# Pinned sums for the conditioning vectors, one operand in PSUM, and weight sums in pieces of 256

## The chip, the cores and the metric

The kernel runs on one core of a Trainium2 chip. The metric is the device time of one execution in microseconds (us). Three timed runs of the kernel before took 3041.25, 3040.60 and 3039.13 us, a median of 3040.6. Line numbers are those of the kernel before, and times within the execution count from the start of its span.

## The reference, cut to what matters

One layer of a denoising backbone runs over 1024 latent and 128 context tokens (1152 columns) of width 1024. Each token passes a first feed-forward half-step, a mixer of attention and a gated scan, and a second feed-forward half-step. Each of the three blocks has a shift, a scale and a gate per channel, nine vectors of 1024 for the latent tokens (from `c`) and nine for the context tokens (from `c_ctx`):

```
mod_p = (jax.nn.silu(c_ctx) @ w_ada[l] + b_ada[l]).reshape(1, N_MOD, D_MODEL)
mod_s = (jax.nn.silu(c) @ w_ada[l] + b_ada[l]).reshape(c.shape[0], N_MOD, D_MODEL)
x = x + 0.5 * m[2] * swiglu(modulate(x, norm_g[0], m[0], m[1]), *ffn1)
x = x + m[5] * mix
x = x + 0.5 * m[8] * swiglu(modulate(x, norm_g[2], m[6], m[7]), *ffn2)
def swiglu(h, w1, w3, w2):
    return (jax.nn.silu(h @ w1) * (h @ w3)) @ w2
```

The products by `w_ada` are matrix-vector products: 9 x 1024 outputs of length 1024, for two vectors. The feed-forward width is 2816, which makes 22 tiles of 128.

## The kernel before, in words

Everything is kept with channels on the partitions and tokens along the free axis. A float32 product is made of three TensorE matmuls on split operands (high by high, high by low, low by high).

Each feed-forward half-step has a way up (`w1`, `w3`, SiLU, product) and a way down (`w2`). In the way up the first tiles (four in the first half-step, three in the second) go through `plain_block`; the rest, 18 and 19 tiles, go through `fast_block`, a scheme with 7 products in place of 8 for each quadrant of weights. This is called the fast stage here. A tile `f` of it has 7 products, each for two column groups (`r`), so 14 blocks of 12 matmuls of 288 columns. Every block ends with an operation on VectorE or ScalarE that empties its PSUM bank (L1544 to L1560). The weights of the 7 products are made in `fast_ops`: GpSimd adds and subtracts 128x512 pieces of the raw weights (L1513, four such sums a tile), ScalarE makes the high part (L1517), VectorE the low part (L1518). Weights are made a few products ahead (the list `made`).

In the way down (`down_group`, `down`), two tiles' weights and hidden values are taken at a time. A group of 24 accumulations (8 output tiles by 3 column chunks of 384) has 6 matmuls for each; VectorE then adds the result, times the gate, to `x` (L481). The PSUM tag `dn` has three banks. ScalarE (L238, L1619) and GpSimd (L239, L1620) split the weights and hidden values of later tiles meanwhile. The last four tiles go through `down_last`.

Conditioning vectors 0 and 1 are made on TensorE at the start. The other seven are made by `ada_sum` on VectorE, beside other work: vectors 2 to 5 in the first fast stage, 6 and 7 in the first way down, 8 in the second fast stage. For each 128x512 block of the transposed `w_ada` (tile `wada`, loaded by L289, two buffers) two SCALAR_TENSOR_TENSOR instructions (L306) multiply it by SiLU of the conditioning row, broadcast over the partitions (tiles `cb`, one for each of the two vectors), and sum along the row into a column of `acc`; a DVE_READ_ACCUMULATOR follows each. This text calls the pair of instructions one sum. There are 128 sums in the first fast stage, 64 in the way down and 32 in the second fast stage.

`ada_sum` is a generator; the loops around it decide where its next step is traced:

```
L1641 if (n in (1, 4)) if l else (7 * f + n) % 3:
L1642     next(ada, None)
```

(after both blocks of product `n`), and in the way down one step after every third accumulation. In the fast stages one step holds both sums of a block of weights; in the way down it holds one. What is traced is not yet the order of the engines: a scheduler orders each engine's queue by its own estimate of when an instruction's operands are there, so an instruction without ties to the work around it can move ahead. `keep_in_program_order` ties an instruction behind the one traced before it on its engine. The queues themselves are in order: SyncE's (SP) issues all the loads and stores named here, and an entry that waits holds those behind it.

Of the kernel before, what the change touches and what calls it, by code (L numbers as in the profile page):

```python
# [9 lines left out]
F32 = mybir.dt.float32  # L10
# [3 lines left out]
AF = mybir.ActivationFunctionType  # L14
ALU = mybir.AluOpType
# [4 lines left out]
P = 128  # L20
D = 1024
# [66 lines left out]
class Trunk:  # L88
# [185 lines left out]
        )  # L274
        self.ada_end(m)

    def ada_sum(self, ms, cb, w2, small, fine=False):

        nc, a = self.nc, self.a
        HD = D // 2  # L280
        acc = small("adac")[:, : 32 * len(ms)].rearrange("p (m h k s) -> p m h k s", m=len(ms), h=2, k=KT)
        junk = small("junk").bitcast(BF16)[:, :HD]
        w2 = w2("wada")
        ws = [w2[:, :HD], w2[:, HD : 2 * HD]]
        units = [(h, i, k) for h in range(2) for i in range(len(ms)) for k in range(KT)]

        def load(n):
            h, i, k = units[n]
            nc.sync.dma_start(ws[n % 2], a["w_aT"][ms[i] - 2, k, :, ts(h, HD)])  # L289

        cs = None
        for n, (h, i, k) in enumerate(units):
            if not i and not k:
                cs = [cb("cb")[:, :HD] for _ in range(2)]
                for s in range(2):
                    nc.sync.dma_start(cs[s], a["cr"][s : s + 1, ts(h, HD)].to_broadcast([P, HD]))
                if not n:
                    load(0)
                for s in range(2):
                    nc.scalar.activation(cs[s], cs[s], AF.Silu)  # L300
                yield
            if n + 1 < len(units):
                load(n + 1)
            for s in range(2):
                o = acc[:, i, h, k, s : s + 1]
                nc.vector.scalar_tensor_tensor(junk, ws[n % 2], 1.0, cs[s], ALU.mult, ALU.mult, accum_out=o)  # L306
                if fine and not s:
                    yield
            if h and k == KT - 1:
                nc.vector.tensor_add(acc[:, i, 0], acc[:, i, 0], acc[:, i, 1])  # L310
                b = self.bada[:, ms[i]].unsqueeze(2).to_broadcast([P, KT, 2])
                nc.vector.tensor_tensor(self.modt[:, ms[i]], acc[:, i, 0], b, ALU.add)
                self.ada_end(ms[i])
            yield
# [1173 lines left out]
    def fast_ops(self, l, fs):  # L1488

        nc = self.nc  # L1490
        raws, n = [None, None], 0

        def load(f, i):
            t = raws[i] = self.wp.tile([P, 2, 512], F32, tag="raw", bufs=2, name="raw")
            for v, (j, h) in enumerate((((0, 0), (1, 0)), ((1, 1), (0, 1)))[i]):
                src = self.a["w13"][l, f, j][:, 4 * h : 4 * h + 4].rearrange("p k m -> p (k m)")
                nc.sync.dma_start(t[:, v], src)

        load(fs[0], 0)
        load(fs[0], 1)  # L1500
        yield
        for j, f in enumerate(fs):
            (a11, a21), (a22, a12) = [(t[:, 0], t[:, 1]) for t in raws]
            s1, s2 = [self.half("ws")[:, :512] for _ in range(2)]
            src = {1: a11, 6: s2, 7: a21, 5: s1, 2: a12, 4: a22, 3: a12}
            pre = {
                6: ((s1, a21, a22, ALU.add), (s2, s1, a11, ALU.subtract)),
                7: ((a21, a11, a21, ALU.subtract),),
                3: ((a12, a12, s2, ALU.subtract),),
            }  # L1510
            for i in PRODUCTS:
                for o, x, y, op in pre.get(i, ()):
                    nc.gpsimd.tensor_tensor(o, x, y, op)  # L1513
                t = self.wp.tile([P, 2, 512], F32R, tag=("wh", "wl")[n % 2], bufs=3, name="wo")
                wh, wl = t[:, 0], t[:, 1]
                n += 1
                nc.scalar.copy(wh, src[i])  # L1517
                nc.vector.tensor_sub(wl, src[i], wh)  # L1518
                if j + 1 < len(fs) and i in (7, 3):
                    load(fs[j + 1], int(i == 3))  # L1520
                yield [w.rearrange("p (k m) -> p k m", k=4) for w in (wh, wl)]
# [42 lines left out]
    def ffn_fast(self, l, gm, nxt):  # L1564

        nc = self.nc
        w2 = self.a["w2"][l]
# [5 lines left out]
        for f in range(plain):  # L1573
            ws = self.pre[f] if l == 0 and f < 2 else [self.load_w(self.a["w13"][l, f, j], KT, P) for j in range(2)]
# [6 lines left out]
            n = 0  # L1581
# [16 lines left out]
        made = [w for w in made if w]  # L1598
        self.B = None
        pend, ws, raws = [], [], []  # L1600
        ada = self.ada_sum((8,) if l else (2, 3, 4, 5), self.half, partial(self.tt, F32), self.slim)
        tile = partial(self.tt, F32) if l == 0 else self.wide
        split = partial(self.wide, dt=F32R) if l == 0 else partial(self.tt, F32R)
        spare = partial(self.tt, F32R) if l == 0 else partial(self.wide, dt=F32R)
# [1 line left out]
        def load_x(k):  # L1606
            t = self.tt(F32, f"x{k}")
            nc.sync.dma_start(t[:, :T], self.xs[k] if l else self.a["xT"][k])
            return t

        def load_h(f):
            raw = tile("hr")[:, :T]
            nc.sync.dma_start(raw, self.hs[f])
            return f, raw

        def split_h(f, raw):
            new = partial(self.tt, F32R) if f in (16, 17) else split
            hh, hl = new(name="hh")[:, :T], new(name="hl")[:, :T]
            nc.scalar.copy(hh, raw)  # L1619
            nc.gpsimd.tensor_sub(hl, raw, hh)  # L1620
            return f, (hh, hl)

        def load_w2(f):
            return self.load_w(w2[f], 1, D, home=spare if f % 2 else None)

        for f in range(plain, NF):
            blocks = [self.fast_block(f, r) for r in range(2)]
            for g in blocks:
                next(g)
            for n in range(7):  # L1630
                if len(made) < 6:
                    w = next(ops, None)
                    if w:
                        made.append(w)
                w = made.pop(0)
                for t in self.puts:
                    self.put(*t)
                self.puts = []
                for g in blocks:
                    g.send(w)  # L1640
                if (n in (1, 4)) if l else (7 * f + n) % 3:  # L1641
                    next(ada, None)  # L1642
                if f == NF - 1:
                    if n == 2:
                        raws = [load_h(0), load_h(1)]
                    elif n == 3:
                        ws.append(load_w2(0))
                        pend.append(split_h(*raws[0]))
                    elif n == 4:
                        pend.append(split_h(*raws[1]))  # L1650
                    elif n == 5:
                        ws.append(load_w2(1))
                        self.x = [load_x(0), load_x(1)]
# [2 lines left out]
            self.put(*t)  # L1656
        self.x += [load_x(k) for k in range(2, KT)]
        if l == 0:
            new = partial(self.tt, F32)
            self.bg = self.ada_sum((6, 7), new, new, self.slim, True)  # L1660
        for f in range(2, NF):
            pend.append(split_h(*load_h(f)))
            if f % 2 and f < NF - 1:
                fs, hs = zip(*pend[:2])
                self.down_group(w2, fs, hs, gm, ws or [load_w2(v) for v in fs])
                pend, ws = pend[2:], None
# [126 lines left out]
```

## Time and profile before

| what | value |
|---|---|
| median of three timed runs | 3040.6 us |
| the profiled execution's own time | 3039.14 us |
| its span, first to last instruction | 3037.4 us |
| mean granted TensorE clock | 0.985 of full speed |
| TensorE matmul busy | 2896.2 us (95%) |
| VectorE busy | 2070.8 us (68%) |
| ScalarE busy | 1233.2 us (41%) |
| GpSimd busy | 1049.2 us (35%) |
| first fast stage | from about 154 to 577 us |
| first way down | from about 577 to 890 us |
| second fast stage | from about 2316 to 2739 us |

TensorE is busy nearly all the time. Time is lost where it waits, and where its granted clock falls, which the records show after some of the waits. The span is 1.7 us shorter than the profiled execution, and that is 1.5 us under the median.

### The profile page before, as it was taken

How to read it: one execution, taken by the hardware profiler on the slowest of the kernel's cores; microseconds unless marked ns; L12 is line 12 of the kernel's file. 1: busy time of each engine (PE TensorE's matmuls, PEld its weight loads, DVE VectorE, ACT ScalarE, POOL GpSimd, SP SyncE). 2: the span in 40 equal slices, each digit the busy share in tenths (PEclk: the TensorE clock that was granted, in tenths of full speed). 3: DMA queues.
4: the chain of work that ended last, by engine and by line, in shares of the span. 5: the costliest groups of instructions: out<-in, count | busy, mean ns of one | idle time of the engine just before them, and what ended most of it. 6: DMA issues, size and time to landing. Idle time of an engine off the chain costs nothing. (4 is left out here: it accounts for less than half of the span.)

```text
span 3037.4 us, 49240 instructions
## 1 busy us (share of the span) xinstructions
PE 2896.2 (95%) x18498; PEld 2743.2 (90%) x18498; DVE 2070.8 (68%) x4206; ACT 1233.2 (41%) x2375; POOL 1049.2 (35%) x831
## 2 busy tenths in 40 slices
PE   7999999989999999999999999989999999999998
PEld 5999999979988988888998778779989999999997
DVE  7787865598668777777636777765675745546665
ACT  5422222211166464555344677751262322332113
POOL 4222222343334233333225444533242222226324
PEclk8999999999999999999999999999999999999999
DMA  6643432553121111111110000143253322226211
GB/s 236 198 152 123 144 108 77 206 198 106 36 96 37 52 38 45 45 45 45 58 60 20 13 17 21 48 149 104 95 188 115 107 75 75 76 93 224 89 44 63
DMA packets 151470, 282.37 MB, mean 93 GB/s; under 512 B 19200, under 2 KB 83648, under 8 KB 151232
## 3 DMA queue, kind: packets, MB, share of 16 engines
q1 hardware_dynamic: 151088, 278.90, 27.7%
q8 instruction: 146, 2.39, 0.3%
q14 instruction: 92, 0.75, 0.1%
q10 hardware_dynamic: 144, 0.33, 0.0%
HBM read 215.64 MB, written 63.52 MB: 92 GB/s over the span
## 5 line engine op out<-in xcount | busy, mean ns | idle before, releaser
L1542 PE MATMUL b<-xo,wo 128*128 128x288 f32 x3552 | 487.1, 297 | 9.6 <-DVE et L1548 9.6
L1542 PEld LDWEIGHTS b<-xo,wo 128*128 128x128 f32 x3552 | 477.3, 189 | 11.5 <-DVE et L1548 11.5
L481 DVE SCALAR_TENSOR_TENSOR x<-dn,modt,x 128x256 f32<-128x256 f32 (+4 forms) x728 | 350.5, 504 | 166.0 <-PE dn L454 164.7
L1542 PE MATMUL b<-bh,wo 128*128 128x288 f32 x1776 | 367.0, 296 | 4.1 <-DVE et L1550 3.2
L239 POOL TENSOR_TENSOR wl<-raw,wh 128x1024 fp32r<-128x1024 f32 (+1 forms) x106 | 241.4, 2278 | 372.9 <-ACT wh L238 357.0
L452 PE MATMUL mm<-xh,wh 128*128 128x384 f32 (+1 forms) x1008 | 362.9, 360 | 5.4 <-DVE q L649 3.1
L454 PE MATMUL mm<-xh,wl 128*128 128x384 f32 (+1 forms) x1008 | 342.9, 340 | 2.0 <-POOL wl L239 1.8
L453 PE MATMUL mm<-xl,wh 128*128 128x384 f32 (+1 forms) x1008 | 343.5, 341 | 0.0
L1542 PEld LDWEIGHTS b<-bh,wo 128*128 128x128 f32 x1776 | 289.9, 189 | 5.8 <-ACT et L1552 5.7
L1542 PE MATMUL b<-bl,wo 128*128 128x288 f32 x888 | 262.2, 295 | 0.0
L452 PE MATMUL dn<-hh,wh 128*128 128x384 f32 (+2 forms) x576 | 199.7, 347 | 23.7 <-DVE x L481 20.7
L306 DVE SCALAR_TENSOR_TENSOR junk<-wada,cb 128x512 bf16<-128x512 f32 x224 | 205.9, 919 | 16.9 <-DMA wada<-in_w_aT 14.5
L238 ACT CAST wh<-raw 128x1024 fp32r<-128x1024 f32 (+1 forms) x108 | 104.3, 967 | 254.8 <-PE dn L453 166.3
L452 PEld LDWEIGHTS mm<-xh,wh 128*128 128x128 f32 (+1 forms) x1008 | 191.1, 190 | 15.3 <-DVE q L649 3.8
L454 PE MATMUL dn<-hh,wl 128*128 128x384 f32 (+2 forms) x576 | 196.0, 340 | 1.0 <-POOL wl L239 1.0
L1517 ACT CAST wo<-raw 128x512 fp32r<-128x512 f32 x185 | 114.0, 622 | 204.1 <-PE b L1542 115.3
L453 PE MATMUL dn<-hl,wh 128*128 128x384 f32 (+2 forms) x576 | 195.4, 339 | 0.0
L454 PEld LDWEIGHTS mm<-xh,wl 128*128 128x128 f32 (+1 forms) x1008 | 190.4, 189 | 3.6 <-POOL wl L239 2.1
L453 PEld LDWEIGHTS mm<-xl,wh 128*128 128x128 f32 (+1 forms) x1008 | 191.6, 190 | 1.6 <-issue 0.4
L1620 POOL TENSOR_TENSOR hl<-hr,hh 128x1152 fp32r<-128x1152 f32 x44 | 120.5, 2747 | 202.9 <-ACT hh L1619 113.6
L1518 DVE TENSOR_TENSOR wo<-raw,wo 128x512 fp32r<-128x512 f32 x185 | 128.2, 694 | 89.6 <-ACT wo L1517 88.9
L1276 POOL TENSOR_TENSOR ehl<-e,ehl 128x512 fp32r<-128x512 f32 x93 | 122.5, 1322 | 141.0 <-ACT ehl L1274 78.2
(384 smaller groups left out, 7140.0 us busy)
## 6 DMA issues: line engine op xcount, KB each, us to landing
raw<-in_w SPq DMA_DIRECT2D x148, 256.0 KB, 2.9
raw<-in_w SPq DMA_DIRECT2D x58, 512.0 KB, 3.6
wada<-in_w_aT SPq DMA_DIRECT2D x112, 256.0 KB, 2.7
hr<-hs SPq DMA_DIRECT2D x44, 576.0 KB, 4.5
hs<-et SPq DMA_DIRECT2D x148, 144.0 KB, 1.7
raw<-in_w_in SPq DMA_DIRECT2D x41, 512.0 KB, 3.5
hb<-hd SPq DMA_DIRECT2D x44, 288.0 KB, 3.5
x<-in_xT SPq DMA_DIRECT2D x16, 576.0 KB, 8.9
```

What stands on the lines that cost most here:

```text
L238: pin(self.nc.scalar.copy(wh, raw))
L239: pin((eng or self.nc.gpsimd).tensor_sub(wl, raw, wh))
L306: nc.vector.scalar_tensor_tensor(junk, ws[n % 2], 1.0, cs[s], ALU.mult, ALU.mult, accum_out=o)
L452: nc.tensor.matmul(ps, wh, xh, start=start and i == 0, stop=False)
L453: nc.tensor.matmul(ps, wh, xl, start=False, stop=False)
L454: nc.tensor.matmul(ps, wl, xh, start=False, stop=stop and i == n - 1)
L481: nc.vector.scalar_tensor_tensor(self.x[m][:, a:b], ps[:, a - lo : b - lo], self.modt[:, gm, m, s : s + 1], self.x[m][:, a:b], ALU.mult, A ...
L1276: eng.tensor_sub(el, e, eh)
L1517: nc.scalar.copy(wh, src[i])
L1518: nc.vector.tensor_sub(wl, src[i], wh)
L1542: nc.tensor.matmul(ps, w[:, k], x[:, k, :QW], start=first, stop=last, skip_group_check=home != i)
L1620: nc.gpsimd.tensor_sub(hl, raw, hh)
```

## The change

The sums are the same sums. Five things differ in how they are queued and where their operand lies.

1. Each sum is tied by `keep_in_program_order` behind what is traced before it on VectorE.
2. `ada_sum` yields after every sum in all three places, so one step is one sum.
3. In the fast stages the step stands after each single block: in the first, after both blocks of products 0, 1, 2 and 4 (8 sums a tile); in the second, after both blocks of products 1 and 4 (4 a tile).
4. In the way down `cb` lies in PSUM, in two of the three banks of the tag `up`, which the way down doesn't use otherwise; the row is loaded into SBUF (`row`) and ScalarE's SiLU writes it to the bank. In the fast stages `cb` stays in SBUF.
5. Each of GpSimd's weight sums of 128x512 becomes two of 128x256.

```diff
-    def ada_sum(self, ms, cb, w2, small, fine=False):
+    def ada_sum(self, ms, cb, w2, small):
...
-                cs = [cb("cb")[:, :HD] for _ in range(2)]
+                cs = [cb() if cb else self.half("cb")[:, :HD] for _ in range(2)]
+                row = [self.half("row")[:, :HD] for _ in range(2)] if cb else cs
                 for s in range(2):
-                    nc.sync.dma_start(cs[s], a["cr"][s : s + 1, ts(h, HD)].to_broadcast([P, HD]))
+                    nc.sync.dma_start(row[s], a["cr"][s : s + 1, ts(h, HD)].to_broadcast([P, HD]))
...
-                    nc.scalar.activation(cs[s], cs[s], AF.Silu)
+                    nc.scalar.activation(cs[s], row[s], AF.Silu)
...
-                nc.vector.scalar_tensor_tensor(junk, ws[n % 2], 1.0, cs[s], ALU.mult, ALU.mult, accum_out=o)
-                if fine and not s:
+                self.tc.keep_in_program_order(
+                    nc.vector.scalar_tensor_tensor(junk, ws[n % 2], 1.0, cs[s], ALU.mult, ALU.mult, accum_out=o)
+                )
+                if not s:
                     yield
...
-                    nc.gpsimd.tensor_tensor(o, x, y, op)
+                    for v in range(2):
+                        c = ts(v, 256)
+                        nc.gpsimd.tensor_tensor(o[:, c], x[:, c], y[:, c], op)
...
-        ada = self.ada_sum((8,) if l else (2, 3, 4, 5), self.half, partial(self.tt, F32), self.slim)
+        ada = self.ada_sum((8,) if l else (2, 3, 4, 5), None, partial(self.tt, F32), self.slim)
...
-                if (n in (1, 4)) if l else (7 * f + n) % 3:
-                    next(ada, None)
+                    if n in ((1, 4) if l else (0, 1, 2, 4)):
+                        next(ada, None)
...
-            new = partial(self.tt, F32)
-            self.bg = self.ada_sum((6, 7), new, new, self.slim, True)
+            self.bg = self.ada_sum((6, 7), lambda: self.bank("up", "cb", D // 2), partial(self.tt, F32), self.slim)
```

TensorE's queue is the same, instruction for instruction, in both kernels. Three places show what moved. The changed kernel's line numbers are 2 to 5 higher: L308 there is L306 here, L484 is L481, L1523 is L1518, and L1551 to L1565 are L1546 to L1560.

VectorE in the second half of a tile of the first fast stage, before: L1518 makes low parts of weights, L1550 to L1558 empty the banks `b` of products into `et`.

```order
L1550 TENSOR_TENSOR et<-b_2112,et 128x288
L1518 TENSOR_TENSOR wo<-raw,wo 128x512
L306 SCALAR_TENSOR_TENSOR junk,adac<-wada,cb 128x512 x4
L1518 TENSOR_TENSOR wo<-ws,wo 128x512
L1554 TENSOR_TENSOR et<-b_2060,et 128x288
L1555 TENSOR_TENSOR et<-et 128x288
L306 SCALAR_TENSOR_TENSOR junk,adac<-wada,cb 128x512
L1554 TENSOR_TENSOR et<-b_2074,et 128x288
L306 SCALAR_TENSOR_TENSOR junk,adac<-wada,cb 128x512
L1555 TENSOR_TENSOR et<-et 128x288
L1518 TENSOR_TENSOR wo<-raw,wo 128x512
L1558 TENSOR_TENSOR et<-b_2098,et 128x288
```

The same stretch of a tile in the changed kernel:

```order
L1555 TENSOR_TENSOR et<-b_2624,et 128x288
L1523 TENSOR_TENSOR wo<-raw,wo 128x512
L1523 TENSOR_TENSOR wo<-ws,wo 128x512
L308 SCALAR_TENSOR_TENSOR junk,adac<-wada,cb 128x512
L1559 TENSOR_TENSOR et<-b_2571,et 128x288
L308 SCALAR_TENSOR_TENSOR junk,adac<-wada,cb 128x512
L1560 TENSOR_TENSOR et<-et 128x288
L1559 TENSOR_TENSOR et<-b_2586,et 128x288
L1523 TENSOR_TENSOR wo<-raw,wo 128x512
L1560 TENSOR_TENSOR et<-et 128x288
L1563 TENSOR_TENSOR et<-b_2610,et 128x288
L1565 TENSOR_TENSOR et<-et 128x288
```

Six sums between the first L1550 and L1558 have become two. Counted over the stage, the sums of the 18 tiles stood as 0, 17, 17, 18, 12, 0, 0, 12, 18, 18, 16 and then none; now they stand as 8 (once 7, once 9) in each of 16 tiles.

VectorE in the first way down, before: the L481 rows are one output tile `x` each, its chunk with the context columns in two pieces (256 and 128) and two chunks of 384.

```order
L306 SCALAR_TENSOR_TENSOR junk,adac<-wada,cb 128x512
L481 SCALAR_TENSOR_TENSOR x_6191<-dn,modt,x_6191 128x256
L481 SCALAR_TENSOR_TENSOR x_6191<-dn,modt,x_6191 128x128
L481 SCALAR_TENSOR_TENSOR x_6191<-dn,modt,x_6191 128x384
L306 SCALAR_TENSOR_TENSOR junk,adac<-wada,cb 128x512
L481 SCALAR_TENSOR_TENSOR x_6191<-dn,modt,x_6191 128x384
L306 SCALAR_TENSOR_TENSOR junk,adac<-wada,cb 128x512
```

The same place in the changed kernel:

```order
L308 SCALAR_TENSOR_TENSOR junk,adac<-wada,cb 128x512
L484 SCALAR_TENSOR_TENSOR x_6263<-dn,modt,x_6263 128x256
L484 SCALAR_TENSOR_TENSOR x_6263<-dn,modt,x_6263 128x128
L484 SCALAR_TENSOR_TENSOR x_6263<-dn,modt,x_6263 128x384 x2
L308 SCALAR_TENSOR_TENSOR junk,adac<-wada,cb 128x512
```

Two sums for each output tile have become one; the last sum moves from the sixth of the nine groups to the ninth.

SP's queue over a tile of the first fast stage, before: `raw` are weights of the way up, `wada` the blocks for the sums, `hs` the stores of finished rows.

```order
L1497 DMA raw<-in_w 128x512 x2
L289 DMA wada<-in_w_aT 128x512 x4
L1497 DMA raw<-in_w 128x512 x2
L289 DMA wada<-in_w_aT 128x512 x2
L1436 DMA hs_631<-et 128x288 x2
L289 DMA wada<-in_w_aT 128x512
L1436 DMA hs_631<-et 128x288 x2
L289 DMA wada<-in_w_aT 128x512 x2
```

The changed kernel's, over a tile:

```order
L1439 DMA hs_631<-et 128x288 x4
L1500 DMA raw<-in_w 128x512 x2
L289 DMA wada<-in_w_aT 128x512 x3
L1500 DMA raw<-in_w 128x512 x2
L289 DMA wada<-in_w_aT 128x512
```

Nine loads of `wada` in such a tile have become four, as its sums become fewer; three of them still stand behind the loads of `raw` of that tile.

## Rows read from the trace of the kernel before

**Rows 1.** The page, its first part: busy time, share of the span, instructions.
```profile
PE 2896.2 (95%) x18498; PEld 2743.2 (90%) x18498; DVE 2070.8 (68%) x4206; ACT 1233.2 (41%) x2375; POOL 1049.2 (35%) x831
```

**Rows 2.** TensorE's waits, 150 to 590 us: us in total, times, longest.
```profile
PE b L1542 <- DVE et L1548: 9.6, 8, 2.4
PE b L1542 <- DVE et L1550: 3.2, 4, 1.7
PE b L1542 <- ACT et L1552: 0.8, 1, 0.8
```

**Rows 3.** TensorE's waits for VectorE, 590 to 820 us.
```profile
PE dn L452 <- DVE x L481: 20.0, 18, 2.6
```

**Rows 4.** Busy time of each engine in stretches, and the granted clock.
```profile
core 0: us, PE busy (x) PEld busy (x) DVE busy (x) ACT busy (x) POOL busy (x), PEclk, DMA share, GB/s
155.00:255.00 100.00, 91.94 (x655) 89.65 (x654) 91.13 (x206) 25.87 (x56) 23.92 (x16) 0.97 0.49 156
255.00:360.00 105.00, 105.00 (x792) 105.00 (x792) 77.53 (x174) 29.41 (x61) 22.75 (x17) 1.00 0.38 125
...
590.00:730.00 140.00, 118.31 (x619) 111.45 (x617) 134.65 (x268) 26.93 (x27) 65.24 (x24) 0.96 0.52 176
730.00:800.00 70.00, 69.99 (x399) 69.99 (x400) 44.44 (x92) 11.68 (x12) 28.04 (x12) 1.00 0.24 71
```

**Rows 5.** The sums alone (L306) in those stretches; each counts twice, with its read.
```profile
155.00:255.00 100.00, 50.16 (x120) 0.97 0.49 156
255.00:360.00 105.00, 27.50 (x72) 1.00 0.38 125
...
590.00:730.00 140.00, 77.99 (x128) 0.96 0.52 176
```

**Rows 6.** One of five stretches of 15 us where the clock falls.
```profile
190.00:205.00 15.00, 12.27 (x79) 11.67 (x79) 11.92 (x31) 2.88 (x6) 4.57 (x3) 0.89 0.43 135
```

**Rows 7.** VectorE's groups by shape, 590 to 820 us: count, busy us, mean ns.
```profile
L306 DVE SCALAR_TENSOR_TENSOR junk<-wada,cb 128x512 bf16<-128x512 f32 x64 | 77.5, 1210 | 1.5 <-DMA wada<-in_w_aT 1.5
L481 DVE SCALAR_TENSOR_TENSOR x<-dn,modt,x 128x384 f32<-128x384 f32 x126 | 77.0, 613 | 24.0 <-PE dn L454 23.6
L481 DVE SCALAR_TENSOR_TENSOR x<-dn,modt,x 128x256 f32<-128x256 f32 x63 | 30.2, 479 | 13.1 <-PE dn L454 12.9
L481 DVE SCALAR_TENSOR_TENSOR x<-dn,modt,x 128x128 f32<-128x128 f32 x63 | 21.4, 339 | 0.0
```

**Rows 8.** VectorE in order of time, at 605 us: start, length.
```profile
605.29 2.62 DVE L306 SCALAR_TENSOR_TENSOR junk<-wada,cb 128x512 bf16<-128x512 f32 x1
```

**Rows 9.** GpSimd in order of time, from 604 us.
```profile
604.97 2.40 POOL L239 TENSOR_TENSOR wl<-raw,wh 128x1024 fp32r<-128x1024 f32 x1 [0.68 <-PE dn L454]
```

**Rows 10.** VectorE from 616 us, while GpSimd's next row runs.
```profile
616.93 0.60 DVE L481 SCALAR_TENSOR_TENSOR x<-dn,modt,x 128x384 f32<-128x384 f32 x1
```

**Rows 11.** GpSimd from 616 us.
```profile
616.96 2.41 POOL L239 TENSOR_TENSOR wxl<-raw,wxh 128x1024 fp32r<-128x1024 f32 x1 [3.43 <-ACT wxh L238]
```

**Rows 12.** The sums from 590 to 820 us: ns min/median/max.
```profile
L306 DVE SCALAR_TENSOR_TENSOR junk<-wada,cb x64: 673/680/3143, 592.6 to 723.5; 128x512 bf16<-128x512 f32 x64
```

**Rows 13.** GpSimd's weight sums, 420 to 575 us, without conditioning sums.
```profile
L1513 POOL TENSOR_TENSOR ws<-raw x6: 1287/1294/1468, 428.5 to 540.1; 128x512 f32<-128x512 f32 x6
```

**Rows 14.** GpSimd's weight sums by shape, 150 to 580 us.
```profile
L1513 POOL TENSOR_TENSOR raw<-raw 128x512 f32<-128x512 f32 x18 | 25.8, 1433 | 0.1
```

**Rows 15.** Who ScalarE waited for, from 150 to 590 us.
```profile
ACT wo L1517 <- POOL ws L1513: 97.5, 17, 9.5
```

**Rows 16.** Who SP's queue waited for, from 150 to 580 us.
```profile
SPq L1497 <- DVE wo L1518: 97.0, 28, 9.4
```

**Rows 17.** Who VectorE waited for, from 150 to 590 us.
```profile
DVE junk L306 <- DMA wada<-in_w_aT: 10.3, 20, 1.8
```

**Rows 18.** The page, its DMA issues: KB each, median us to landing.
```profile
wada<-in_w_aT SPq DMA_DIRECT2D x112, 256.0 KB, 2.7
```

**Rows 19.** The second fast stage's stretch with its 32 sums (columns as in Rows 4).
```profile
2320.00:2417.00 97.00, 97.00 (x734) 97.00 (x733) 69.28 (x152) 27.97 (x57) 22.13 (x17) 1.00 0.37 119
```

## The prediction

> **What bounds the kernel now.** I read the page's first part, then TensorE's waits by stretch, then what VectorE and GpSimd do in the stretches with waits. The page shows TensorE busy for 95% of the span [rows 1], and TensorE's queue is the same in both kernels. So the change can only give back TensorE's waits, and what its clock loses after them.
>
> In the first fast stage TensorE waits 9.6 + 3.2 + 0.8 = 13.6 us for banks that VectorE or ScalarE has not emptied [rows 2]. In the first way down it waits 20.0 us for L481 [rows 3]. The stretches show where: from 155 to 255 us TensorE is busy for 91.9 of 100 us, from 590 to 730 us for 118.3 of 140; from 255 to 360 us, and after 730 us, it is full [rows 4]. The sums alone divide the time the same way. They number 60, 36 and 64 in the first three of these stretches (half the counts, as each comes with its read) [rows 5], and the last one in the way down is at 723.5 us [rows 12]. So the waits are where the sums are dense.
>
> After some waits the clock falls. [...] One costs (1 - 0.89) x 15 = 1.65 us: 3.3 us in the fast stage and 5.0 in the way down. The whole to be had is 13.6 + 3.3 + 20.0 + 5.0 = 41.9 us.
>
> **The fast stage: pinning and spreading.** A tile takes 168 matmuls; by the full stretch (792 in 105 us) that is 22.3 us. Without sums VectorE has 10.6 us of work a tile: 77.5 us from 255 to 360 less 27.5 of sums leaves 50.0 over 105 / 22.3 = 4.7 tiles [rows 4, 5]. A sum costs 50.16 / 60 = 0.84 us in the dense stretch and 27.5 / 36 = 0.76 in the thin one. With 17 sums a tile VectorE has 10.6 + 17 x 0.84 = 24.9 us to do in 22.3, so it falls behind by 2.6 us a tile. Product 4 adds on in the bank of product 7, and product 3 in that of product 5, both five blocks later, so L1548 and L1550 may be 5 x 22.3 / 14 = 8 us late; past that TensorE waits, and for these two lines it does. With 8 a tile VectorE has 10.6 + 8 x 0.8 = 17.0 us in 22.3, and 5.3 us are left for waits on weights. The stretch from 255 to 360 us is the nearest row: it holds tiles with 12 sums and with none, VectorE is 74% busy and TensorE never waits. The second fast stage with its 32 sums in 97 us waits for nothing either [rows 19], so spreading them there gives nothing.
>
> The new cost is that a pinned sum stands in VectorE's queue until its block of weights lands. What is queued behind it is the emptying of the next bank, and TensorE waits for that if it is 8 us late. A load lands 2.7 us after issue [rows 18]. In the order, most blocks of weights have three blocks of matmuls (4.8 us) between the buffer coming free and its use, one in each tile only two (3.2 us), which leaves 0.5 us. I expect VectorE to stand 1 to 2 us a tile there, inside its 5.3. I give back 2 us of the 16.9 for the start of the stage. Bounds: 0 regained, if the waits have another cause, to 16.9.
>
> **The way down: spreading and PSUM.** A sum takes 0.68 us at the median, but 1.21 on average and 3.14 at worst [rows 7, 12]. In order of time one sees why: a sum starts at 605.29, GpSimd has been reading SBUF since 604.97, and the sum ends at 607.91, 0.54 us after GpSimd's 607.37 [rows 8, 9]. L481 starting at 616.93, with a GpSimd sum of 2.41 us starting at 616.96, takes 0.60 us, its usual time [rows 10, 11, 7]. Both have float32 operands; the sum reads two from SBUF, L481 one from SBUF and one from PSUM. So with `cb` in PSUM I expect a sum not to stop for GpSimd. That saves VectorE 64 x (1.21 - 0.68) = 34 us of stops.
>
> Its own price is not in the trace. L481 grows from 339 to 479 to 613 ns over 128, 256 and 384 elements [rows 7], 1.07 ns an element, so 512 take about 750 ns; the lower bound is 680 (no price), the upper 1210 (the stops stay). I take 750, since L481 has the same kinds of operand. [...]
>
> An accumulation of 6 matmuls takes 70 / 399 x 6 = 1.05 us; VectorE has 2.04 us for three (128.6 us over 63) and now one sum of 0.83 with its read: 2.87 of 3.16 us if nothing overlapped, 63% + 24% = 87% by the full stretch, where L481's instructions overlap a little [rows 4, 7]. TensorE can run two accumulations (2.1 us) ahead of L481, since `dn` has three banks; one sum of 0.83 fits, one of 2.5 did not. What is late next: VectorE at 87% has little room if a block of `wada` is late, because SP stands before weights of `w2` whose buffer GpSimd must release first. I keep 4 us of the 25.0 for that, about 0.4 for each of nine groups. Bounds: 0 to 25.0.
>
> ScalarE's SiLU into the bank, two rows for each half of the channels, I cost at nothing: ScalarE has 26.9 of 140 us to do there [rows 4], and without that room a row would cost at most about a sum's 0.68 us.
>
> **GpSimd's pieces.** A sum of 512 takes 1.29 us undisturbed [rows 13], one of 1024 takes 2.40 [rows 9], so 2.17 ns an element and 0.18 us fixed: a piece of 256 takes 0.74, a pair 1.48, 0.19 more. Four a tile make 0.76 us on an engine that is idle most of the stage. The chain of two that ScalarE waits for gets 0.38 longer; ScalarE already waits 97.5 / 17 = 5.7 us for it without TensorE waiting in most of those tiles [rows 15]. I take 0; below zero it can only give VectorE shorter stops (L1518 and others still read two SBUF operands), worth at most what is left of the waits.
>
> [...]
>
> **Sum.** 16.9 - 2 + 25.0 - 4 = 35.9 us. The profiled execution of 3039.1 becomes 3003.2; the runs' median of 3040.6 becomes 3004.7. I forecast 3005 us, its own range 2998 to 3014.
>
> **Rivals.** (A) Only the way down gains: in the fast stage VectorE is late because weights are late (ScalarE stands 5.7 us for them), not because of the sums. For it: the longest waits of ScalarE are up to 9.5 us. Against: the same waits without TensorE waiting where sums are thin. 3040.6 - 21 = 3020.
>
> (B) Only the fast stage gains: a sum with one operand in PSUM still stops for GpSimd, or 87% is too full. Against: L481 beside GpSimd. The spreading alone would still halve the density. 3040.6 - 15 = 3026, less what that gives.
>
> (C) The pieces come onto the path: 37 tiles of both fast stages x 0.76 us = 28 us eat most of the gain, 3005 + 28 = 3033. [...]
>
> (D) Slower: the pinned sum holds VectorE behind a late block of weights in every tile. SP's queue puts three `wada` behind `raw`, for which it stood up to 9.4 us [rows 16]. A load released so would land 9.4 + 2.7 = 12.1 us late, 4.1 past the 8 us that a bank can wait: 16 tiles x 4.1 = 66 us, and none of the fast stage's gain, so 3040.6 - 21 + 66 = 3086. It is slower than before from 21 / 16 = 1.3 us a tile, a block 9.3 us late each time. Against: SP's 97.0 us of these waits are 28, 3.5 us on average, and VectorE stood 10.3 us for `wada` in the whole stage, 1.8 at most [rows 17].
>
> **How the numbers follow.** Forecast 0.70; A 0.10; B 0.10; C 0.04; D 0.06. A measurement of this kernel tells about 0.2%, 6 us, from no change. The forecast, A and B are faster, C at 3033 lies by the edge of 3034.5, so I count 0.03 of its 0.04 as the same and 0.01 as faster: faster 0.70 + 0.10 + 0.10 + 0.01 = 0.91, same 0.03, slower 0.06. The range from 2997 (all 41.9 us and the spread of runs, 2 us) to 3026 holds the forecast, A and half of B, which lies at its edge, and leaves out the rest, 0.15.
>
> **What would show it.** In the profile after: no sum in the way down over about 0.9 us, mean near 0.75, whatever GpSimd does; sums from about 165 to 530 us and from 590 to 790; waits of TensorE for L1548 and L1550 under 3 us in all and for L481 under 6; the clock at full speed from 150 to 590 and with at most one fall from 590 to 820; GpSimd's pieces near 0.74 us; VectorE's waits for `wada` up, to 10 to 30 us, without TensorE behind them. I am wrong if TensorE's waits in the two stretches add up to more than 15 us, or if they are at other lines in the same places.

## The result and the profile after

The changed kernel takes 2990.4 us (median of five runs, 2987.7 to 2992.0) against 3040.6; the ratio is 0.9834, 95% interval 0.982 to 0.9849. It is 50.2 us faster. Forecast were 3005 us, a gain of 35.6, with a range from 2997 to 3026: the direction was right, the size too small.

The page's first part for the changed kernel, to be read against [rows 1]:

```profile
PE 2882.2 (96%) x18498; PEld 2737.8 (92%) x18498; DVE 2034.1 (68%) x4206; ACT 1242.1 (42%) x2375; POOL 1084.1 (36%) x979
```

TensorE is busy for 14.0 us less with the same instructions. The forecast had asked for 8.3 of that, for the clock; matmuls that restart after a wait are longer too (0.44 us in place of 0.34 in e9 below), and there are fewer of both.

Who TensorE waited for, first from 150 to 560 us and then from 560 to 800 us (us in total, times, longest), against [rows 2, 3]:

```profile
PE b L1547 <- ACT et L1557: 0.7, 1, 0.7
...
PE dn L457 <- POOL wl L239: 1.0, 1, 1.0
PE dn L455 <- DVE x L484: 0.9, 2, 0.6
```

The waits for L1553 and L1555 (L1548 and L1550 before) are gone, the one for L1557 (L1552 before) stays at 0.7 us, and those for L484 fell from 20.0 to 0.9 us. The stretches that answer to [rows 4], all engines:

```profile
150.00:250.00 100.00, 99.26 (x747) 99.03 (x746) 77.65 (x169) 34.28 (x68) 34.48 (x40) 1.00 0.42 139
250.00:350.00 100.00, 100.00 (x755) 100.00 (x754) 74.08 (x165) 29.70 (x58) 32.35 (x38) 1.00 0.38 125
...
560.00:700.00 140.00, 139.02 (x795) 138.13 (x794) 109.63 (x263) 30.84 (x30) 70.80 (x28) 1.00 0.56 192
700.00:790.00 90.00, 88.99 (x510) 88.67 (x509) 67.35 (x161) 11.68 (x12) 28.05 (x12) 1.00 0.22 72
```

VectorE is now 74 to 78% busy in these four stretches, where it was 91% and 96% in the two dense ones. The clock is 1.00, and TensorE is all but full. VectorE in the way down by shape, against [rows 7], and the sums' least, median and longest ns, against [rows 12]:

```profile
L484 DVE SCALAR_TENSOR_TENSOR x<-dn,modt,x 128x384 f32<-128x384 f32 x144 | 88.7, 617 | 44.8 <-PE dn L457 44.7
L308 DVE SCALAR_TENSOR_TENSOR junk<-wada,cb 128x512 bf16<-128x512 f32 x64 | 43.4, 678 | 1.3 <-DMA wada<-in_w_aT 1.3
```
```profile
L308 DVE SCALAR_TENSOR_TENSOR junk<-wada,cb x64: 677/677/689, 572.1 to 767.8; 128x512 bf16<-128x512 f32 x64
```

The longest sum fell from 3143 to 689 ns, the mean from 1210 to 678, and the 384-column addition is as long as before: the stops are gone, not moved to it. Counted by TensorE's groups of 144 matmuls, the sums of the way down lay in the first five (7, 16, 16, 15 and 10); now they lie in all nine (6, 8, 8, 8, 7, 8, 8, 8 and 3).

**Where the time came from.** TensorE's queue is the same in both kernels and in all runs below but one, e9, where nine of the 18,498 matmul rows (numbers 18,215 to 18,223) stand elsewhere. So a stage can be timed from the start of one matmul to the start of another, the same two each time: numbers 1000 to 4000 for the first fast stage, 4000 to 5200 for the way down, counted from zero. Each kernel has one profiled execution, and the table is read from it:

| kernel | fast stage us | way down us | rest of the span us |
|---|---|---|---|
| before | 421.2 | 242.3 | 2373.9 |
| changed | 401.6 | 210.6 | 2377.2 |
| e1 pieces alone | 425.3 | 243.5 | 2376.6 |
| e2 PSUM operand alone | 421.7 | 224.6 | 2379.3 |
| e3 pins alone | 401.0 | 228.1 | 2378.3 |
| e4 changed, `cb` in SBUF | 402.0 | 231.1 | 2371.8 |
| e5 changed, pieces of 512 | 402.4 | 210.4 | 2376.7 |
| e6 changed, no pins | 427.0 | 225.8 | 2377.8 |
| e7 changed, 19 or 20 sums a tile | 434.7 | 210.7 | 2374.9 |

The change gained 19.6 us in the fast stage and 31.6 in the way down, 51.2 together. The rest lies between 2371.8 and 2379.3 in all nine, without an order by what was changed, so I take its 3.3 us for scatter. The size of the scatter in the two stages can be seen in e8 to e10 below, which leave both as in the changed kernel: 401.9 to 404.2 us and 210.2 to 210.5.

### The profile page after: what moved, and what is told of

It is laid out like the page before. It is cut to its first block, busy times and chain, and to the rows that moved or that the text cites. A ratio compares the mean times of both kernels' runs of the same rounds, so it can differ in the third digit from the quotient of the medians.

```text
span 2989.4 us, 49363 instructions
## 1 busy us (share of the span) xinstructions
PE 2882.2 (96%) x18498; PEld 2737.8 (92%) x18498; DVE 2034.1 (68%) x4206; ACT 1242.1 (42%) x2375; POOL 1084.1 (36%) x979
## 5 line engine op out<-in xcount | busy, mean ns | idle before, releaser
L484 DVE SCALAR_TENSOR_TENSOR x<-dn,modt,x 128x256 f32<-128x256 f32 (+4 forms) x728 | 353.2, 505 | 167.9 <-PE dn L457 167.0
L1523 DVE TENSOR_TENSOR wo<-raw,wo 128x512 fp32r<-128x512 f32 x185 | 127.1, 688 | 102.2 <-ACT wo L1522 99.3
L1518 POOL TENSOR_TENSOR ws<-raw 128x256 f32<-128x256 f32 x74 | 68.5, 945 | 292.9 <-DMA raw<-in_w 265.8
```

Of the source, the lines that this page charges most:

```text
L484: nc.vector.scalar_tensor_tensor(self.x[m][:, a:b], ps[:, a - lo : b - lo], self.modt[:, gm, m, s : s + 1], self.x[m][:, a:b], ALU.mult, A ...
L1518: nc.gpsimd.tensor_tensor(o[:, c], x[:, c], y[:, c], op)
```

## The experiments

**e1, the pieces alone.** The kernel before with

```diff
-                    nc.gpsimd.tensor_tensor(o, x, y, op)
+                    for v in range(2):
+                        c = ts(v, 256)
+                        nc.gpsimd.tensor_tensor(o[:, c], x[:, c], y[:, c], op)
```

> The kernel before with one edit: GpSimd's weight sums of 512 become two of 256. The order of the sums stays dense (17 or 18 a tile in the first fast stage, 14 to 16 a group in the way down). My theory (the gain is from spreading the sums and from the PSUM operand; the pieces are worth nothing): within 4 us of 3040.6, TensorE's waits in the first fast stage stay between 11 and 16 us. Rival (shorter holds by GpSimd let VectorE keep up, and that is where the gain beyond the forecast came from): the fast stage's waits fall under 9 us and the time is 3034 or less. Rival C of the prediction (pieces on the path): 3045 or more.

Measured: ratio 1.0011 (1.0002 to 1.0021), 3 us slower. The fast stage is 4.1 us longer, with 17.6 us of waits for L1550, L1552 and L1554 (L1548, L1550 and L1552 before), over the 16 expected at most. The pieces did not bring the extra gain; whether they cost 3 us, as rival C has it, e5 settles.

**e2, the PSUM operand alone.** The kernel before with `row` loaded into SBUF and SiLU written to two banks:

```diff
-            self.bg = self.ada_sum((6, 7), new, new, self.slim, True)
+            self.bg = self.ada_sum((6, 7), lambda n: self.bank("up", n, D // 2), new, self.slim, True)
```

> The kernel before with one edit: cb lies in PSUM in the way down. The sums stay dense, 14 a group of 24 accumulations in place of 8. Theory 1 (stops behind GpSimd made the waits): no sum over 0.7 us, L481's waits under 4 us, and nearly all of the way down's 31.6 us is gained: 3009 to 3013. Theory 2 (density made them): per output tile VectorE has 2.04 us of L481 and two sums of 0.76, 3.55 in 3.16 us; over 35 output tiles it falls behind by about 14 us less what the banks cover, so some 12 us of waits stay and the time is 3022 to 3030.

Measured: 3026.1 us, ratio 0.9944 (0.9927 to 0.9961). The way down gains 17.6 of the 31.6 us. TensorE's waits in it, then the sums:

```profile
PE dn L453 <- DVE x L482: 8.7, 6, 3.2
```
```profile
L307 DVE SCALAR_TENSOR_TENSOR junk<-wada,cb x64: 673/677/689, 592.1 to 712.0; 128x512 bf16<-128x512 f32 x64
```

No sum is stopped any more, and still TensorE waits, 8.7 us where theory 2 expected some 12. But density did not make these waits as theory 2 has it. VectorE kept up with 14 sums in a group, for it stood waiting for TensorE 30 times (586 to 725 us, VectorE's waits):

```profile
DVE x L482 <- PE dn L455: 9.6, 30, 1.2
DVE junk L307 <- DMA wada<-in_w_aT: 8.9, 5, 4.2
```

Three of TensorE's waits, 0.6, 0.8 and 3.1 us, end just after VectorE stood for a late block of `wada`. The longest of these stands (VectorE in order of time) goes back to SP, which stood 6.8 us before a load of `w2` until GpSimd was done (SP's waits, 680 to 697 us):

```profile
694.73 0.69 DVE L307 SCALAR_TENSOR_TENSOR junk<-wada,cb 128x512 bf16<-128x512 f32 x1 [4.21 <-DMA wada<-in_w_aT]
```
```profile
SPq L244 <- POOL wl L239: 6.8, 1, 6.8
```

Two more, 3.2 and 0.7 us, come after the last steps on the finished vectors. These are tiny, 0.16 us undisturbed, and were stopped three times in a row, each with a GpSimd instruction running beside it (the third, L322, took 2.01 us):

```profile
713.09 2.63 DVE L311 TENSOR_TENSOR adac<-adac 128x16 f32<-128x16 f32 x1
715.76 2.26 DVE L313 TENSOR_TENSOR modt<-adac,vec 128x16 f32<-128x16 f32 x1
```

The sixth, 0.2 us, lies before the sums. So theory 1 fails, as waits stay; theory 2 had the size right by luck and the mechanism wrong. By the traces, what spreading removes here are late blocks, the event that the forecast kept 4 us for, and badly timed last steps. The operands of these steps are as they were: in the changed kernel the first of them (L313) took 0.42 and 0.52 us, having started 0.4 and 0.5 us before an instruction of GpSimd ended.

**e3, the pins alone.** The kernel before with

```diff
-                nc.vector.scalar_tensor_tensor(junk, ws[n % 2], 1.0, cs[s], ALU.mult, ALU.mult, accum_out=o)
+                self.tc.keep_in_program_order(
+                    nc.vector.scalar_tensor_tensor(junk, ws[n % 2], 1.0, cs[s], ALU.mult, ALU.mult, accum_out=o)
+                )
```

> The kernel before with one edit: each sum is pinned behind what is traced before it. In the order this alone spreads them: 8 or 10 a tile in the first fast stage, 7 or 8 a group in the way down. cb stays in SBUF, the steps and the pieces stay as before. The fast stage gives its whole 20 us if density is the cause there, also with both sums of a block in one step. In the way down, theory 1 (stops): sums up to 3.1 us stay, about 18 GpSimd sums lie there, and L481's waits stay at 8 to 15 us: 3000 to 3008. Theory 2 (density): the room between sums absorbs the stops, waits under 4 us: 2990 to 2996.

Measured: 3007.5 us, ratio 0.9885 (0.9866 to 0.9904). The fast stage gets all of its gain (401.0 us), with two sums in a step and pieces of 512. In the way down the spreading alone gains 14.1 us; the sums still stop, and TensorE still waits, also for VectorE's last step on a finished vector (L314), which is queued behind them and once behind a step (L312) stopped for 1.9 us:

```profile
L307 DVE SCALAR_TENSOR_TENSOR junk<-wada,cb x64: 672/683/3016, 572.2 to 782.5; 128x512 bf16<-128x512 f32 x64
```
```profile
PE dn L454 <- DVE x L483: 8.0, 9, 1.9
PE dn L454 <- DVE modt L314: 4.4, 2, 3.0
```

So each edit gives about half of the way down: 17.6 us from the operand alone, 14.1 from the spreading alone, and 31.6 with both. With the stops in place the order does decide how far VectorE falls behind: it is busy for 120.1 us from 575 to 715, where it was busy for 134.65 of 140 [rows 4].

**e4, the changed kernel with `cb` in SBUF in the way down.**

```diff
-            self.bg = self.ada_sum((6, 7), lambda: self.bank("up", "cb", D // 2), partial(self.tt, F32), self.slim)
+            self.bg = self.ada_sum((6, 7), lambda: self.tt(F32, "cb")[:, : D // 2], partial(self.tt, F32), self.slim)
```

> The changed kernel with cb in SBUF in the way down, all else as in it. The way down's order is that of the changed kernel, so it differs by the stops alone. Theory 1 (stops): the sums' mean is 1.0 us or more, L484's waits 8 to 15 us, 3000 to 3008. Theory 2 (density): waits under 4 us, 2990 to 2995, the same as the changed kernel.

Measured: 3013.0 us (four runs, 3007.1 to 3017.6), ratio 0.9903 (0.988 to 0.9925); the profiled execution's span is 3005.0. VectorE's order in the way down is that of the changed kernel, instruction for instruction; the stage is 20.5 us longer, with 10.8 us of waits for L484 and sums of 1.13 us on average and up to 3.04. Theory 1 holds here, though the time is 5 us over its band, and the place of one operand is worth those 20.5 us even when the sums are spread. In both kernels 36 of the 64 sums ran beside an instruction of GpSimd. Why e4 takes 3 us more there than e3 stays open; the intervals overlap.

**e5, the changed kernel with pieces of 512** (the edit of e1 undone).

> The changed kernel with GpSimd's weight sums in one piece of 512, all else as in it. Theory (the pieces are worth nothing, since pinning alone emptied the fast stage's waits without them): 2988 to 2993, no difference from the changed kernel's 2990.4. Rival (the pieces cost, as e1 came out 4 us slower in its fast stage): 2985 to 2988. Rival (the pieces help VectorE): 2993 to 2998.

Measured: 2989.4 us, ratio 0.983 (0.9817 to 0.9844): the same as the changed kernel's 0.9834. The pieces are worth nothing, either way. GpSimd's weight sums in the changed kernel by shape, 150 to 560 us:

```profile
L1518 POOL TENSOR_TENSOR ws<-raw 128x256 f32<-128x256 f32 x36 | 35.5, 1006 | 152.4 <-DMA raw<-in_w 128.8 <-DVE bl L1396 23.6
L1518 POOL TENSOR_TENSOR ws<-ws,raw 128x256 f32<-128x256 f32 x36 | 33.1, 938 | 0.0
L1518 POOL TENSOR_TENSOR raw<-raw,ws 128x256 f32<-128x256 f32 x36 | 27.4, 781 | 136.0 <-issue 129.5 <-ACT cb L301 6.5
L1518 POOL TENSOR_TENSOR raw<-raw 128x256 f32<-128x256 f32 x36 | 26.6, 759 | 0.0
```

Together 122.6 us, where e5's 72 sums of 512 take 28.9 + 28.8 + 25.1 + 24.6 = 107.4: the pieces cost 15.2 / 18 = 0.84 us a tile on GpSimd, near the 0.76 forecast, and TensorE waits for none of it: its one wait there is the 0.7 us for L1557.

**e6, the changed kernel without its pins** (the edit of e3 undone).

> The changed kernel without the pins; the steps, the PSUM operand and the pieces stay. In the order the sums gather again, 17 or 18 a tile and 14 a group. Theory (the pin spreads the sums, the steps by themselves do nothing): the fast stage as in the kernel before, about 20 us over the changed one, the way down as in the run with the PSUM operand alone, 14 us over it: 3022 to 3030. Rival (the finer steps matter in themselves): under 3012.

Measured: 3031.6 us (ratio 0.9967, 0.9954 to 0.9979), with the waits back in the fast stage: 6.9 us for L1553, 6.7 for L1551, 2.1 for L1555 (L1550, L1548 and L1552 in the kernel before). The time is 2 us over the expected band; the fast stage is 5.8 us longer than in the kernel before. The finer steps by themselves do not spread the sums: the scheduler gathers them again, 17 to 20 in each of three tiles and 14 in a group. The waits of the way down are of the kinds of e2, four after late blocks and one after the last steps.

**e7, more sums a tile, pinned.**

```diff
-                    if n in ((1, 4) if l else (0, 1, 2, 4)):
+                    if n in ((1, 4) if l else (0, 1, 2, 4, 5)):
                         next(ada, None)
+                        if not l:
+                            next(ada, None)
```

> The changed kernel with more sums a tile in the first fast stage: two after each block of products 0, 1, 2, 4 and 5, 19 or 20 a tile over 6.5 tiles, pinned as before. Theory (density makes the waits): VectorE has 10.6 + 19.5 x 0.78 = 25.8 us to do in a tile of 22.3, falls 3.5 us a tile behind, 23 us over the 6.5 tiles, of which the first 8 are covered: about 15 us of waits at L1551 and L1553, and 18 to 25 us longer with restarts and clock: 3008 to 3016. Rival (the waits came from late weights or from sums that had moved to bad places, and pins alone cured them): no waits, 2988 to 2994.

Measured: 3022.2 us, ratio 0.9939 (0.9926 to 0.9953). Who TensorE waited for in the fast stage, and VectorE for `wada`:

```profile
PE b L1547 <- DVE et L1555: 18.4, 7, 3.6
PE b L1547 <- DVE et L1553: 3.5, 4, 2.1
```
```profile
DVE junk L308 <- DMA wada<-in_w_aT: 12.6, 18, 2.3
```

More sums a tile, with every sum pinned in its place, bring the waits back, 21.9 us against the 15 expected, mostly at L1555 and none at L1551; the time is 6 us over the expected band. VectorE stood 12.6 us for blocks of `wada`, which that estimate had left out; I did not test that this makes the whole difference. The stage is 33.1 us longer, more than its waits by half, as in the kernel before.

**e8, e9, e10: what a wait costs.** The gain of 51.2 us was larger than all that the forecast had seen to be had, 41.9. Three kernels add waits to the second way down, which has two short ones of 1.3 us together. Before the addition of a chosen accumulation VectorE repeats it into a scratch tile (the output is unchanged):

```diff
+        for _ in range(getattr(self, "late", 0)):
+            t = self.half("late")[:, : hi - lo]
+            nc.vector.scalar_tensor_tensor(t, ps, self.modt[:, gm, m, 0:1], self.x[m][:, cs], ALU.mult, ALU.add)
...
+                self.late = 9 if gm == 8 and c == 1 and m in (3,) else 0
```

with 9 copies once a group (e8), 6 twice (e10), 4 four times (e9).

> The changed kernel with nine extra instructions on VectorE (copies of the addition L484, 128x384 from PSUM, into a scratch tile) before one addition in each of the nine groups of the second way down, which had no waits there. Each makes TensorE wait once for about 9 x 0.61 - 1.4 = 4.1 us, 37 us in all. Theory (each wait costs 0.28 us beyond the idle time that the trace shows, whatever its length): beside the clock, 9 x 0.28 = 2.5 us more than the idle time. Rival (the excess goes with the idle time, as in before: 11.6 us on 35.2, less the clock's 8.3): the idle time's tenth or more, 4 us and up.

> As e8, but four extra instructions before four additions in each group: 36 waits of about 4 x 0.61 - 1.4 = 1.0 us, 37 us in all again. Theory (a price for each wait): beside the clock, 36 x 0.28 = 10 us more than the idle time, four times that of e8. Rival (the excess goes with the idle time): as much as in e8.

> As the two runs with added waits, with six extra instructions before two additions in each group: 18 waits of about 2.15 us by their slope (1.11 at four, 3.72 at nine). Theory (0.27 a wait beside the clock): 18 x 0.27 = 4.8 us beyond the idle time if the clock never falls, 4.8 + 18 x 1.72 = 36 if it falls after each. The fall came after none of 35 waits of 1.1 and after each of nine of 3.7; in the kernel before after some of about 2. I expect it after some of the 18.

Measured, one run each (e8 3039.5, e9 3041.9 and e10 3056.2 us), against the changed kernel, matmul by matmul. The stage is the second way down, numbers 16,900 to 18,400, or one of the two stages of the kernel before. Waits and idle time are those that the changed kernel doesn't have; idle is from the modelled end of one matmul to the start of the next; "falls" are drops of the granted clock to its lower level (0.50 in the kernel before, from 198 to 200 us), at which the matmuls of 384 columns in e8 start 0.32 us apart in place of 0.174:

| stage | waits | idle us | stage longer by us | beyond idle | falls |
|---|---|---|---|---|---|
| e9 | 35 of 1.1 us | 38.7 | 48.1 | 9.4 | 0 |
| e10 | 18 of 2.2 us | 38.8 | 63.6 | 24.8 | 13 |
| e8 | 9 of 3.7 us | 33.5 | 49.8 | 16.3 | 9 |
| before, fast stage | 12 | 12.9 | 19.6 | 6.7 | 2 |
| before, way down | 18 | 21.0 | 31.6 | 10.6 | 3 |

The stretch with most of these waits in e9, then in e8 (columns as in [rows 4]); the granted clock is the last column but two:

```profile
2735.00:2985.00 250.00, 215.77 (x1186) 205.69 (x1186) 187.56 (x387) 31.93 (x35) 75.52 (x33) 1.00 0.17 58
```
```profile
2735.00:2985.00 250.00, 220.20 (x1176) 217.34 (x1174) 160.28 (x328) 32.17 (x35) 73.46 (x33) 0.95 0.16 57
```

In e9 the clock never falls in this stage, so its 9.4 us over 35 waits are a price of the wait itself, 0.27 us. The timeline of TensorE around one of them shows where it lies (start, length):

```profile
2757.92 0.34 PE L455 MATMUL dn<-hh,wxh 128*128 128x384 f32 x1
2758.09 0.34 PE L456 MATMUL dn<-hl,wxh 128*128 128x384 f32 x1
2758.27 0.34 PE L457 MATMUL dn<-hh,wxl 128*128 128x384 f32 x1
2759.71 0.44 PE L455 MATMUL dn<-hh,wh 128*128 128x384 f32 x1 [1.11 <-DVE x L487]
2760.00 0.33 PE L456 MATMUL dn<-hl,wh 128*128 128x384 f32 x1
2760.17 0.34 PE L457 MATMUL dn<-hh,wl 128*128 128x384 f32 x1
```

Here a matmul starts every 0.17 us and lasts 0.34, so records overlap by half. From 2758.27 to 2759.71 are 1.44 us, 1.27 more than one spacing, of which the profile calls only 1.11 idle; and the first matmul after the wait takes 0.29 us to its successor, 0.11 more. 0.16 + 0.11 = 0.27.

In e8 the same price is 9 x 0.27 = 2.4 us; the other 13.9 are nine falls of the clock, 1.54 us each. One of them in the timeline of TensorE:

```profile
2739.96 0.49 PE L455 MATMUL dn<-hh,wh 128*128 128x384 f32 x1 [3.71 <-DVE x L487]
2740.25 0.52 PE L456 MATMUL dn<-hl,wh 128*128 128x384 f32 x1
2740.57 0.52 PE L457 MATMUL dn<-hh,wl 128*128 128x384 f32 x1
...
2743.45 0.42 PE L457 MATMUL dn<-hh,wxl 128*128 128x384 f32 x1
2743.71 0.34 PE L455 MATMUL dn<-hh,wh 128*128 128x384 f32 x1
2743.88 0.34 PE L456 MATMUL dn<-hl,wh 128*128 128x384 f32 x1
```

Twelve matmuls take 3.75 us from 2739.96 to 2743.71, against 12 x 0.174 = 2.09 at full speed: 1.66 more, of which 0.11 are the restart in the first. The two prices, taken from e9 and e8, give 18 x 0.27 + 13 x 1.54 = 24.9 us for e10, which has 24.8. The rival (an excess that goes with the idle time) falls: a price of 9.4 / 38.7 = 0.24 for each us of idle time leaves 0.91 for a fall in e8, and 21.3 us for e10. The interval across a wait alone is longer than idle time and spacing by 0.16 us in each of the three kernels, with waits of 1.1, 2.2 and 3.7 us. e8 missed as it was put, since its "beside the clock" is 2.4 us only once nine falls are taken off, and I had not expected one after each wait; e10's expectation had a fall at 1.72 us, too high.

## Why the prediction was wrong

The mechanisms that the forecast named were right in the fast stage and for the stops; the step that failed is the term "The whole to be had is 13.6 + 3.3 + 20.0 + 5.0 = 41.9 us", which has no price for the restart after a wait, and after it the 6 us kept back. Against the 51.2 us measured in the two stages:

| | forecast us | measured us |
|---|---|---|
| idle time of the waits | 33.6 | 33.9 |
| clock after them | 8.3 | 7.5 |
| restarts, 30 waits | 0 | 8.3 |
| kept back for the start and late blocks | -6.0 | 0 |
| not placed | 0 | 1.5 |
| sum | 35.9 | 51.2 |

- **Waits and clock** were read correctly. The 8.3 us for the clock are five falls of 1.65 us. Beside the one of [rows 6] the kernel before has these four, one more in the fast stage and three in the way down (columns as in [rows 4]):

```profile
245.00:260.00 15.00, 12.67 (x81) 11.88 (x80) 14.48 (x32) 2.88 (x6) 4.56 (x3) 0.89 0.49 159
590.00:605.00 15.00, 12.44 (x63) 12.15 (x62) 12.35 (x25) 4.33 (x5) 7.64 (x4) 0.89 0.72 253
645.00:660.00 15.00, 12.65 (x61) 12.07 (x62) 13.79 (x29) 0.67 (x1) 4.62 (x2) 0.89 0.56 185
705.00:720.00 15.00, 11.35 (x53) 10.60 (x53) 14.66 (x29) 2.31 (x2) 9.17 (x4) 0.89 0.41 136
```

  Matmul by matmul, those that ran at the lower clock were 7.5 us longer than in the changed kernel, 1.5 for each of the five falls, as in e8. The 1.5 us not placed lie in other matmuls.
- **Restarts** were missing. I took the waits' idle time as their whole cost and TensorE's busy time as work. The intervals across the 30 waits and the first matmuls after them were 8.3 us longer beyond the idle time, 0.28 a wait, close to the 0.27 of e9. A table of waits alone gives the bound too low by that, here a fifth of the 41.9.
- **The reserves** were not needed. 2 us were for the start of the fast stage, where the first stretch has 99.3 of 100 us. The other 4 were for late `wada` in the way down: VectorE stood there once, for 1.3 us. The danger was real, though: it makes half of the waits that are left in e2. In the fast stage I expected 10 to 30 us of such standing; it fell from 10.3 [rows 17] to one of 2.1 us:

```profile
DVE junk L308 <- DMA wada<-in_w_aT: 2.1, 1, 2.1
```

- **The fast stage's arithmetic** (2.6 us a tile behind at 17 sums, room at 8) is borne out from both sides, by e3 and, in direction, by e7. What spreads them is the pin, not the finer step (e6). The forecast worked on the order and did not part the two.
- **The way down**: the operand and the spreading each gave about half (e2, e3). The forecast gave one figure for both. Its reading of the stops was right; with them gone, what spreading still gains (14.0 us from e2 to the changed kernel) hangs on late blocks and last steps, not on a VectorE that can't keep up. Its load of 87% was worked out with a slip, since 0.83 of 3.16 us are 26% and not 24%; the stretch from 560 to 700 us has 78%.
- **The PSUM operand's price** was put at 0.75 us a sum, 70 ns over the 680, my estimate from L481's lengths [rows 7]; measured it is 0.677 against a median of 0.680 with both operands in SBUF [rows 12], so none. That the sums then don't stop for GpSimd was right: in the changed kernel and in e2 36 of the 64 ran beside an instruction of GpSimd, and none took over 689 ns.
- **The pieces** cost GpSimd 0.84 us a tile and the kernel nothing, as forecast. Measured they are 122.6 / 144 = 0.85 us on average, 0.11 over the 0.74 worked out for one alone, which is the median of three of the four shapes: 8 x 0.11 = 0.9 us a tile.
- **The rivals**: A and B fall with both stages' gains; C with e5; D with VectorE's waits for `wada`, 2.1 us in the whole fast stage, where D needed a block about 9 us late in every tile.

Of what was to show it, the waits, the clock and the sums' length came as said, and the sums lie from 165 to 510 us and from 572 to 768. The pieces took 0.85 us in place of 0.74, and VectorE's waits for `wada` went down in place of up.

None of the runs beats the changed kernel: e5 is its equal with two lines less.

## What to carry to other kernels

When waits of an engine with overlapping instructions go, price them from start to start: idle time, plus a fixed restart for each wait (0.27 us here), plus the clock where it falls after them (1.5 us a fall here). Work that fills an engine's gaps stayed spread here only where each instruction was tied to its place; without the ties the scheduler moved the sums forward in bunches (17 to 20 in each of three tiles in e6). The count per tile must fit the room that the other work leaves: with 8 pinned sums TensorE waited 0.7 us in the fast stage, with 19 or 20 it waited 21.9 us for VectorE (e7). With one operand in PSUM side work on VectorE was out of GpSimd's way (no sum over 689 ns, against up to 3039 in e4); that and the spreading each gave half, and an experiment with one part alone was needed to tell. When some waits are left in such a run, look at each of them: in e2 their sum fitted a theory that their causes did not.

## What the runs showed of the hardware that was not expected

- In e9 a TensorE wait cost 0.27 us more than its idle time with the clock at full speed throughout (35 waits of 1.1 us, 9.4 us).
- The granted clock fell after none of 35 waits of 1.1 us (e9), after 13 of 18 of 2.2 us (e10) and after all nine of 3.7 us (e8), 1.5 us lost each time. So the same 33 to 39 us of waiting cost 48, 64 and 50 us; the middle size was the dearest.
- A SCALAR_TENSOR_TENSOR of 128x512 with an accumulator took 677 ns at the median with its second operand in PSUM and 680 with it in SBUF, and in PSUM it never took over 689 beside GpSimd's instructions, against 3143.
- Small steps of VectorE with two float32 operands in SBUF were stopped about as long as the sums, whose longest took 3143 ns against 680 at the median: three of 128x16, 0.16 us undisturbed, took 2.63, 2.26 and 2.01 us beside GpSimd in e2.
